# Combining the experts' rows earlier and reordering the context's last layer in a two-block transformer

## The chip, the cores and the metric

The kernel runs on one core of a Trainium2 chip. The metric is the device time of one execution in microseconds (us). Everything is computed in float32 by splitting each operand into a high and a low part and adding three products, so each weight block is cast once (ScalarE) and its remainder taken once (VectorE, DVE) before TensorE (PE) uses it.

## The reference

Two blocks follow each other on 512 tokens of width 1024. The first ends with a mixture of experts: a router picks two of sixteen experts for each token, each expert is a gated feed-forward, and the two results are added with the token's weights.

```python
def expert_block(args):
    xblk, e = args
    return (jax.nn.silu(xblk @ w1[e]) * (xblk @ w3[e])) @ w2[e]
yb = lax.map(expert_block, (xb, blk_e)).reshape(P, D)
out = jnp.zeros((N + 1, D), f32).at[row_tok].add(yb.astype(f32) * row_w[:, None])
...
x = x + hierarchical_moe(h, ...)
return rms_norm(x, g_final)
```

The second block has two layers over these 512 tokens and a context of 256 tokens. Each layer projects the latent tokens and the context with the same weights, mixes by three kinds of attention (neighbourhood attention, gated linear attention, grouped-query attention), and adds a feed-forward. The latent tokens need the context's keys, values and final states of the same layer. After the last layer the context itself is not needed, so in it the context yields keys, values and states alone:

```python
for l in range(DEPTH_2):
    ctx_out = l < DEPTH_2 - 1
    ...
    if ctx_out:
        xc = layer_norm(...)   # attention and feed-forward of the context
return x
```

## The kernel before, in words

The context doesn't depend on the first block. `moe` (L1164) therefore runs two instruction streams side by side: the foreground is the context's layer 0 (`layer2(0, stc, None, True)`, L1187), the background is a Python generator `experts` (L1177) that routes and then computes the sixteen experts. Each time the foreground has prepared a weight block (`wchunk`, L385), `pump` (L318) advances the background by `rate` steps, 1.85 here; a step of an expert is one 512 KB weight block with its six matmuls, and an expert has twelve. What the generator's steps and the foreground emit is the order of the program; the tile framework then issues instructions by readiness with that order as priority, waits for tiles that are still in use, and keeps each engine's queue in order.

The two streams have their own weight buffers: the experts four raw blocks and three split blocks, the context's layer 0 two and two (`Stream("c", ring, 2, 2, 2, 2, 512)`, L1185). The feed-forward of the context (`ffn`, L2101) has 66 weight blocks: for each of the first two factors 22 blocks of 128 hidden columns, and 22 blocks of the output projection, in groups of 4, 4, 4, 4, 2 and 4 times 128 hidden columns. Its layer norm follows the last block; `hT_tile` (L490) transposes the rows, applies scale and shift and splits them.

Then the context's layer 1 (`layer2(1, stc, None, False)`, L1196) runs as the foreground, with `combine` (L1201) behind it as the background at one step per weight block. `combine` loads the four row tiles of the tokens on SyncE's queue (SP), gathers each token's two expert rows from DRAM (eight indirect transfers on GpSimd's queue), adds them on DVE (`add`, L1221), takes the norm on ScalarE, writes the transposed tile of the main stream (`rest`, L1228), multiplies the rows on GpSimd and stores them on SP's queue. The gathers read `yd`, so they wait for the last expert's store (L1454).

In layer 1 the context runs, in the order of the program: gated linear attention (`gla`, L1830: gate projection, decay chain with exponentials, logarithms and scans, keys, values, states), grouped-query keys (128 columns) and values (128 columns) in two projections (L1721, L1723), neighbourhood values (`na_v`, L1577), and three blocks of neighbourhood keys (`na`, `na_kq`). Keys, values and states are stored to DRAM for the main stream, on SP's queue. Then the main stream's layer 0 begins with the gate projection of its own `gla`.

Tiles that matter: `pj` is a projection of tokens, `pf` of features, `fab` the feed-forward's first two factors, `h` and `yps` an expert's products, `raw`, `w_h`, `w_l` a weight block and its parts, `hT_h` and `hT_l` transposed inputs, `yg` a gathered row tile, `xmoe` the tokens' rows, `gfin` a row of gains.

## Time and profile before

| | |
|---|---|
| median of 3 runs | 2645.08 us (2640.8 to 2653.45) |
| the profiled execution | 2653.58 us, of which its span is 2651.8 us |
| PE busy | 2481.3 us, 94% |
| DVE busy | 1700.1 us, 64% |
| ScalarE busy | 1281.5 us, 48% |
| DMA | 436.54 MB, 165 GB/s on average |
| mean granted clock of PE | 0.963 of full |

A matmul's busy time overlaps with its neighbour's; the distance from start to start is what one costs. The clock that the throttle grants PE has two levels, 1.2 and 2.4 GHz, and a stretch's number is the mean of both over it. A releaser in brackets is the wait that came last before an instruction that found its engine idle.

### The profile page before, as it was taken

The page shows a single profiled execution, that of the slowest core. Times are in us where ns is not written, and L with a number is a line of the kernel's source. Part 1 is how long each engine was busy: PE and PEld are TensorE (multiplying, and loading weights), DVE is VectorE, ACT ScalarE, POOL GpSimd, SP SyncE. Part 2 cuts the span into 40 slices and gives each one's busy share as a digit, 9 for nine tenths or more (in the row PEclk, how much of TensorE's full clock was granted, in tenths as well). Part 3 has the DMA queues.
Part 4 walks back from the last instruction along what each step waited for, and adds up shares of the span by engine and source line. Part 5 has one row for each costly group of instructions (what it writes and reads, how often), then busy time and mean ns, then how long its engine had stood idle before and what let it go on. Part 6 is the DMA issues. An engine that isn't in the chain of part 4 may idle for free.

```text
span 2651.8 us, 35923 instructions
## 1 busy us (share of the span) xinstructions
PE 2481.3 (94%) x13176; PEld 1962.2 (74%) x13176; DVE 1700.1 (64%) x3145; ACT 1281.5 (48%) x2389; POOL 359.2 (14%) x306
## 2 busy tenths in 40 slices
PE   8899899888898999989989999999989899999997
PEld 5547575667677888877876588888868766888886
DVE  3355645787777777877876565444567876644446
ACT  4343445477755665656757642222266574422221
POOL 1100000110001000012230023111142300421101
PEclk9999899899999999988999999999989899999999
DMA  7764347489787898867254224333323524233331
GB/s 276 210 215 147 124 163 269 136 271 302 265 280 242 272 300 279 272 234 224 57 160 128 91 66 127 96 96 99 102 88 97 156 77 135 66 104 100 96 96 64
DMA packets 354132, 436.54 MB, mean 165 GB/s; under 512 B 20384, under 2 KB 228128, under 8 KB 353952
## 3 DMA queue, kind: packets, MB, share of 16 engines
q1 hardware_dynamic: 348000, 412.70, 48.9%
q0 software_dynamic: 5952, 21.50, 2.6%
q8 instruction: 105, 1.72, 0.3%
q14 instruction: 75, 0.61, 0.1%
HBM read 387.21 MB, written 38.01 MB: 160 GB/s over the span
## 4 chain that ended last, share of the span: by engine, by line
PE 46%; DVE 4%; ACT 2%; issue 1%; POOL 1%; DMA 1%; DVEq 0%; ACTq 0%; POOLq 0%
PE fab L345 18%; PE pj L345 17%; PE oat L637 3%; PE pf L345 3%; PE ptp L577 2%; PE sc L544 1%; PE sc L545 1%; PE glG L1983 1%; DMA nab<-in_nabias 1%; POOL x L2081 0%; PE tp L502 0%; DVE w_l L353 0%; ACT pga L663 0%; POOL x L2080 0%; ACT ht L510 0%
## 5 line engine op out<-in xcount | busy, mean ns | idle before, releaser
L353 DVE TENSOR_TENSOR w_l<-raw,w_h 128x1024 fp32r<-128x1024 f32 (+2 forms) x530 | 682.8, 1296 | 452.2 <-ACT w_h L352 443.3
L352 ACT CAST w_h<-raw 128x1024 fp32r<-128x1024 f32 (+2 forms) x530 | 528.3, 1005 | 824.8 <-PE pj L345 279.2
L345 PE MATMUL fab<-hTf_h,w_h 128*128 128x512 f32 (+1 forms) x1104 | 382.4, 348 | 3.6 <-ACT hTf_h L516 3.0
L345 PE MATMUL fab<-hTf_l,w_h 128*128 128x512 f32 (+1 forms) x1104 | 382.7, 347 | 0.2
L345 PE MATMUL fab<-hTf_h,w_l 128*128 128x512 f32 (+1 forms) x1104 | 382.7, 348 | 0.2 <-DVE w_l L353 0.2
L345 PE MATMUL pj<-w_l,hT_h 128*128 128x512 f32 (+3 forms) x608 | 228.7, 377 | 11.3 <-DVE w_l L353 11.3
L345 PE MATMUL pj<-w_h,hT_h 128*128 128x512 f32 (+3 forms) x608 | 221.6, 376 | 12.7 <-ACT w_h L352 7.7
L345 PEld LDWEIGHTS fab<-hTf_h,w_h 128*128 128x128 f32 x1104 | 209.7, 190 | 32.1 <-ACT hTf_h L516 3.4
L345 PEld LDWEIGHTS fab<-hTf_h,w_l 128*128 128x128 f32 x1104 | 209.6, 190 | 28.0 <-DVE w_l L353 0.4
L345 PEld LDWEIGHTS fab<-hTf_l,w_h 128*128 128x128 f32 x1104 | 209.8, 190 | 27.7 <-DVE hTf_l L517 0.6
L345 PE MATMUL pj<-w_h,hT_l 128*128 128x512 f32 (+3 forms) x608 | 224.5, 371 | 0.0
L389 POOL TENSOR_TENSOR raw<-raw,g2b 128x1024 f32<-128x1024 f32 x44 | 113.5, 2588 | 478.7 <-DMA raw<-in_w_ffn_out 437.9
L345 PEld LDWEIGHTS pj<-w_h,hT_h 128*128 128x128 f32 x608 | 119.0, 198 | 42.7 <-issue 14.3
L345 PEld LDWEIGHTS pj<-w_l,hT_h 128*128 128x128 f32 x608 | 120.8, 199 | 39.4 <-DVE w_l L353 16.5
L345 PE MATMUL pj<-w_l,wk_h 128*128 128x512 f32 x376 | 146.2, 390 | 0.5 <-DVE w_l L353 0.5
L345 PE MATMUL pj<-w_h,wk_h 128*128 128x512 f32 x376 | 145.3, 390 | 0.2 <-DVE gps L2072 0.2
L345 PE MATMUL pj<-w_h,wk_l 128*128 128x512 f32 x376 | 143.5, 390 | 0.0
L345 PE MATMUL pf<-hT_h,w_h 128*128 128x512 f32 (+3 forms) x376 | 132.3, 353 | 7.9 <-ACT pT L579 2.9
L345 PEld LDWEIGHTS pj<-w_h,hT_l 128*128 128x128 f32 x608 | 120.6, 198 | 20.9 <-issue 5.2
L345 PE MATMUL pf<-hT_l,w_h 128*128 128x512 f32 (+3 forms) x376 | 130.4, 347 | 2.0 <-DVE hT_l L517 2.0
L345 PE MATMUL pf<-hT_h,w_l 128*128 128x512 f32 (+3 forms) x376 | 130.2, 347 | 0.0
L579 ACT COPY pT<-ptp 128x512 f32<-128x512 f32 (+3 forms) x184 | 88.1, 498 | 55.0 <-PE ptp L577 53.9
(602 smaller groups left out, 4845.5 us busy)
## 6 DMA issues: line engine op xcount, KB each, us to landing
raw<-in_w SPq DMA_DIRECT2D x192, 512.0 KB
raw<-in_w_ffn_in SPq DMA_DIRECT2D x132, 512.0 KB
raw<-in_w_ada SPq DMA_DIRECT2D x96, 512.0 KB
raw<-in_w_in SPq DMA_DIRECT2D x76, 512.0 KB
raw<-in_w_ffn_out SPq DMA_DIRECT2D x66, 512.0 KB
raw<-in_w_out SPq DMA_DIRECT2D x32, 512.0 KB
yd<-ysb SPq DMA_DIRECT2D x16, 512.0 KB
raw<-in_w_in SPq DMA_DIRECT2D x16, 384.0 KB
```

The source lines that it names most:

```text
L345: self.nc.tensor.matmul(out, lhsT=l, rhs=r, start=first and k == 0 and i == 0, stop=last and k == n - 1 and i == 2, **kw)
L352: nc.scalar.copy(out=hl.hi, in_=src)
L353: nc.vector.tensor_sub(out=hl.lo, in0=src, in1=f32(hl.hi))
L389: self.nc.gpsimd.tensor_tensor(out=raw, in0=raw, in1=row.unsqueeze(1).to_broadcast([P, kt, n]), op=OP.mult)
L544: self.nc.tensor.matmul(o, lhsT=q, rhs=k.hi, start=True, stop=False)
L545: self.nc.tensor.matmul(o, lhsT=q, rhs=k.lo, start=False, stop=True)
L577: self.behind = nc.tensor.transpose(tp[:, b * P:(b + 1) * P], st["p"][:, (b0 + b) * P:][:, :P], self.ident)
L579: nc.scalar.copy(out=pT()[:, slice(b0, b0 + bb), ts], in_=tp[:, :bb * P].rearrange("p (b t) -> p b t", t=P))
L637: self.nc.tensor.matmul(st["o"][64 * hh:64 * hh + 64, cols_], lhsT=v(hh), rhs=pT(hh), start=n == 0, stop=n == len(terms) - 1, skip_group_c ...
L1983: nc.tensor.matmul(G[w * c:w * c + w, g0:g0 + GL_H * w].rearrange("p (h t) -> p h t", t=w), lhsT=xk[:, k0:k0 + w], rhs=qb[:, i, :, q0:q0 + ...
```

## The change

The diff does four things. `combine` becomes the tail of the experts' generator: its row loads go to GpSimd's queue, its rows lie in the buffers of the experts' inputs and its gathered rows in `hg` and a small new pool, and additions, norm and the first scaling happen there. The rest (`block2_input`: transposed tiles, multiplication, stores, the last on GpSimd's queue) stays behind the context's layer 1, beginning with the eleventh step. While a background runs, the rate in the feed-forward rises from 1.85 to 2.3. For the context's last layer the order becomes neighbourhood values, neighbourhood keys, the gates of `gla` up to the scans, grouped-query keys and values (called from within `gla`), then the keys, values and states of `gla`. And in that layer the grouped-query keys and values come from one projection of 256 columns. Other layers keep their order.

```diff
@@ -1180,6 +1180,7 @@
                 for e in range(NEXP):
                     yield from self.expert(hd, idx[:, e:e + 1], A["w1"][e], A["w3"][e], A["w2"][e],
                                            yd[e * P:(e + 1) * P, :], ep)
+                yield from self.combine(st, yd, posi, ew, ep)
             ex = Stream("", self.ring, 4, 3, 2, 1, 1024, parts=self.wparts)
             with self.background(ex, experts(), 1.85):
                 self.S = Stream("c", ring, 2, 2, 2, 2, 512)
@@ -1189,8 +1190,7 @@
         self.core_tile(st, 4)
         with self.mirrored():
             with self.psum("psc"):
-                with tc.tile_pool(name="moec", bufs=1, side="left", reuse_waits="tile") as cp, \
-                        self.background(Stream("c", None, 0, 0, 2, 0, 0), self.combine(st, yd, posi, ew, ep, cp), 1.0):
+                with tc.tile_pool(name="moec", bufs=1, side="left", reuse_waits="tile") as cp,                         self.background(Stream("c", None, 0, 0, 2, 0, 0), self.block2_input(st, cp), 1.0):
                     self.S = Stream("", self.ring, 4, 3, 4, 2, 512, parts=self.wparts)
                     self.pump()
                     ctxd.append(self.layer2(1, stc, None, False, keep_hT=True))
@@ -1198,42 +1198,52 @@
         self.S = self.main
         return ctxd
 
-    def combine(self, st, yd, posi, ew, ep, cp):
+    def combine(self, st, yd, posi, ew, ep):
+
+        nc, tc = self.nc, self.tc
+        xs = st["xs"] = []
+        with tc.tile_pool(name="moey", bufs=1, side="left", reuse_waits="tile") as cy:
+            ys = []
+            for i in range(4):
+                x = ep.tile([P, D], F32, name="x", tag=("ehT_h", "ehT_l")[i // 2], bufs=2)
+                nc.gpsimd.dma_start(out=x, in_=st["xd"][i * P:(i + 1) * P, :])
+                xs.append(x)
+            for i in range(4):
+                for k in range(2):
+                    pool, tag = ((ep, "hg"), (cy, "yg"))[i % 2]
+                    y = pool.tile([P, D], F32, name="yg", tag=tag, bufs=2)
+                    nc.gpsimd.indirect_dma_start(out=y, out_offset=None, in_=yd,
+                                                 in_offset=bass.IndirectOffsetOnAxis(ap=posi[k][:, i:i + 1], axis=0))
+                    ys.append(y)
+                yield
+                if i > 0:
+                    self.combined(i - 1, xs, ys, ew)
+            yield
+            self.combined(3, xs, ys, ew)
+
+    def combined(self, i, xs, ys, ew):
+        x = xs[i]
+        for k in range(2):
+            self.nc.vector.scalar_tensor_tensor(out=x, in0=ys[2 * i + k], scalar=ew[k][:, i:i + 1], in1=x, op0=OP.mult, op1=OP.add)
+        r = self.rms_rstd(x.unsqueeze(1), 1, junk=ys[2 * i])
+        self.nc.scalar.mul(x, x, r)
+
+    def block2_input(self, st, cp):
 
         nc = self.nc
         s, t = self.mod_cols(st["ada"][0][1], 1, 0, 0, self.c("vpack", "g_final"), None, "md0", self.cst)
+        g = self.bcast_row(cp, 1, "gfin")
         xd = self.dr.tile([T1, D], F32, name="xd")
-        xs, ys = [], []
+        xs = st["xs"]
+        for _ in range(10):
+            yield
         for i in range(4):
-            x = cp.tile([P, D], F32, name="x", tag="x", bufs=4)
-            nc.sync.dma_start(out=x, in_=st["xd"][i * P:(i + 1) * P, :])
-            xs.append(x)
-            for k in range(2):
-                tag, bufs = (("hg", 2), ("hg", 2), ("ehT_h", 2), ("ehT_h", 2), ("ehT_l", 2), ("ehT_l", 2), ("ysb", 1))[len(ys)] \
-                    if len(ys) < 7 else ("yg", 1)
-                y = (ep if len(ys) < 7 else cp).tile([P, D], F32, name="yg", tag=tag, bufs=bufs)
-                nc.gpsimd.indirect_dma_start(out=y, out_offset=None, in_=yd,
-                                             in_offset=bass.IndirectOffsetOnAxis(ap=posi[k][:, i:i + 1], axis=0))
-                ys.append(y)
+            self.hT_tile(xs[i], i, st["hT"], s, t, cp)
+            yield
+        for i in range(4):
+            nc.gpsimd.tensor_tensor(out=xs[i], in0=xs[i], in1=g, op=OP.mult)
+            nc.gpsimd.dma_start(out=xd[i * P:(i + 1) * P, :], in_=xs[i])
         st["xd"] = xd
-        g = self.bcast_row(cp, 1, "gfin")
-
-        def add(i):
-            x = xs[i]
-            for k in range(2):
-                nc.vector.scalar_tensor_tensor(out=x, in0=ys[2 * i + k], scalar=ew[k][:, i:i + 1], in1=x, op0=OP.mult, op1=OP.add)
-            r = self.rms_rstd(x.unsqueeze(1), 1, junk=ys[2 * i])
-            nc.scalar.mul(x, x, r)
-
-        def rest(i):
-            self.hT_tile(xs[i], i, st["hT"], s, t, cp)
-            nc.gpsimd.tensor_tensor(out=xs[i], in0=xs[i], in1=g, op=OP.mult)
-            nc.sync.dma_start(out=xd[i * P:(i + 1) * P, :], in_=xs[i])
-        for _ in range(6):
-            yield
-        for f, i in ((add, 0), (add, 1), (rest, 0), (add, 2), (rest, 1), (add, 3), (rest, 2), (rest, 3)):
-            f(i)
-            yield
 
     def overflow(self, hd, yd, posf, ovi, pool, ep):
 
@@ -1718,9 +1728,19 @@
             t = sq()
             nc.scalar.activation(t, qk[:, i], AF.Square)
             nc.vector.reduce_sum(ss[:, i * nh:(i + 1) * nh], t, axis=AX.X)
-        self.proj_tok(hT, nt, W[:, c0:c0 + nh * 64], ev)
         v = keep.tile([P, nt, P], F32, name="gav")
-        self.proj_tok(hT, nt, W[:, 2464:2592], lambda i, c0, n, ps: self.copy(v[:, i, :], ps[:, :n]))
+
+        def ev_v(i, _, n, ps):
+            self.copy(v[:, i, :], ps[:, :n])
+
+        def ev_kv(i, _, n, ps):
+            ev(i, _, P, ps)
+            ev_v(i, _, P, ps[:, P:])
+        if full:
+            self.proj_tok(hT, nt, W[:, c0:c0 + nh * 64], ev)
+            self.proj_tok(hT, nt, W[:, 2464:2592], ev_v)
+        else:
+            self.proj_tok(hT, nt, W[:, c0:2592], ev_kv)
         mid = between()
         r = self.rsqrt(ss, nt * nh, 1.0 / 64, 1e-6).rearrange("p (t h) -> p t h", h=nh)
         if full:
@@ -1827,7 +1847,7 @@
             return units
         return attend, mid
 
-    def gla(self, l, hT, T, W, ctxd, full, d, late, pool):
+    def gla(self, l, hT, T, W, ctxd, full, d, late, pool, within):
 
         nc, A = self.nc, self.A
         nt = T // P
@@ -1862,6 +1882,8 @@
         reset = self.c("cpack", "reset")[:, :T]
         nc.vector.tensor_tensor_scan(bs[0], reset, bs[0], 0.0, OP.mult, OP.add)
         nc.vector.tensor_tensor_scan(bs[1][:, ::-1], reset, bs[1][:, ::-1], 0.0, OP.mult, OP.add)
+        if not full:
+            within()
         q = pool.tile([P, T], F32, name="glq")
         k = pool.tile([P, T], F32, name="glk")
 
@@ -2165,15 +2187,22 @@
             hT = lambda k: hTt[:, k, :]
             nes = ExitStack()
             g0, bias = {}, []
-            with tpool("gqp") as p2, tpool("gll") as p0:
+            with tpool("gqp") as p2, ExitStack() as pes:
+                if not full:
+                    vd = self.na_v(l, hT, T, W, p2)
+                    with tpool("nap") as p:
+                        self.na(l, hT, T, W, ctxd, full, d, vd, p, p, g0, (), bias)
+                p0 = pes.enter_context(tpool("gll"))
                 with tpool("glp") as p1:
-                    finish = self.gla(l, hT, T, W, ctxd, full, d, p0, p1)
+                    finish = self.gla(l, hT, T, W, ctxd, full, d, p0, p1,
+                                      lambda: self.gqa(l, hT, T, W, ctxd, full, d, keep, p2, lambda: None, iter(())))
                 p3 = nes.enter_context(tpool("na0", side=self.far)) if lat else None
                 if lat:
                     self.na_bias(l, p3, bias)
                     g0["kc"] = self.fetch(ctxd["na_k"][0], p3, "nakc", bufs=2)
                 begun = self.na_kq(0, l, hT, T, W, lat, full, p3, g0, d) if lat else iter(())
-                attend, vd = self.gqa(l, hT, T, W, ctxd, full, d, keep, p2, lambda: self.na_v(l, hT, T, W, p2), begun)
+                if full:
+                    attend, vd = self.gqa(l, hT, T, W, ctxd, full, d, keep, p2, lambda: self.na_v(l, hT, T, W, p2), begun)
                 self.call(finish)
             oes = ExitStack()
             rows, cols_ = st["ada"][l]
@@ -2209,12 +2238,12 @@
                     self.pipeline(units + [(lambda: switch(s0), *rest)] + more, steps=5)
                 gr, lg, lb = lnr
             else:
-                with tpool("nap") as p:
-                    self.na(l, hT, T, W, ctxd, full, d, vd, p, p, g0, begun, bias)
                 if not full:
                     if not keep_hT:
                         st["hes"].close()
                     return d
+                with tpool("nap") as p:
+                    self.na(l, hT, T, W, ctxd, full, d, vd, p, p, g0, begun, bias)
                 with tpool("gqa") as p:
                     self.pipeline(attend(oT, p))
         with tpool("xx") as px:
@@ -2273,6 +2302,9 @@
                     self.affine(x[:, i, :], x[:, i, :], lg, lb)
                     nc.sync.dma_start(out=xd[i * P:(i + 1) * P, :], in_=x[:, i, :])
                 later = []
+                if self.bg is not None:
+
+                    self.rate = 2.3
                 self.ffn(l, lambda k: hTf[:, k, :], T, x, gr, wk, done2)
                 if later:
                     self.behind_input(st["hT"], lp, later)
```

## Rows read from the trace of the kernel before

**Rows 1.** Page: busy time by engine; granted TensorE clock in 40 equal slices
```profile
PE 2481.3 (94%) x13176; PEld 1962.2 (74%) x13176; DVE 1700.1 (64%) x3145; ACT 1281.5 (48%) x2389; POOL 359.2 (14%) x306
PEclk9999899899999999988999999999989899999999
```

**Rows 2.** Windows: length, engine busy (instructions), PEclk, DMA share, GB/s
```profile
813.80:1152.65 338.85, 337.18 (x2011) 297.03 (x2009) 264.15 (x299) 201.21 (x249) 6.11 (x6) 1.00 0.84 276
1152.65:1169.12 16.47, 9.10 (x45) 6.78 (x43) 15.03 (x40) 9.13 (x17) 0.00 (x0) 0.90 0.57 178
1169.12:1182.40 13.28, 11.59 (x76) 10.37 (x76) 3.97 (x6) 2.43 (x5) 7.66 (x8) 0.86 0.95 329
1182.40:1206.80 24.40, 21.11 (x97) 20.43 (x97) 20.64 (x55) 17.80 (x37) 0.42 (x1) 0.51 0.40 128
1206.80:1239.16 32.36, 27.24 (x192) 25.35 (x193) 32.10 (x68) 22.54 (x45) 14.10 (x8) 1.00 0.76 228
```

**Rows 3.** Waits of PE, 1152.65 to 1239.2: us in total, times, longest
```profile
PE pj L345 <- DVE w_l L353: 4.9, 4, 2.1
PE tp L502 <- DVE x L2061: 4.1, 1, 4.1
PE pf L345 <- ACT hT_h L516: 2.1, 1, 2.1
PE pf L345 <- DVE hT_l L517: 2.0, 1, 2.0
PE pj L345 <- issue: 1.7, 1, 1.7
```

**Rows 4.** Timeline of PE (start, duration, shape): one pair of neighbours per shape and clock
```profile
1184.42 0.41 PE L345 MATMUL pj<-w_h,hT_l 128*128 128x256 f32 x1
1184.64 0.41 PE L345 MATMUL pj<-w_h,hT_h 128*128 128x256 f32 x1
1195.23 0.41 PE L345 MATMUL pj<-w_l,hT_h 128*128 128x128 f32 x1
1195.44 0.41 PE L345 MATMUL pj<-w_h,hT_l 128*128 128x128 f32 x1
...
1208.84 0.27 PE L345 MATMUL pj<-w_l,hT_h 128*128 128x128 f32 x1
1208.95 0.28 PE L345 MATMUL pj<-w_h,hT_l 128*128 128x128 f32 x1
...
1214.96 0.34 PE L345 MATMUL pj<-w_l,hT_h 128*128 128x384 f32 x1
1215.13 0.33 PE L345 MATMUL pj<-w_h,hT_l 128*128 128x384 f32 x1
1226.07 0.28 PE L345 MATMUL pf<-hT_l,w_h 128*128 128x256 f32 x1
1226.19 0.28 PE L345 MATMUL pf<-hT_h,w_l 128*128 128x256 f32 x1
```

**Rows 5.** DVE groups, 1152.65 to 1241.2: xcount, busy, mean ns; one meeting with POOL
```profile
L1224 DVE SCALAR_TENSOR_TENSOR x<-yg,ew,x 128x1024 f32<-128x1024 f32 x8 | 10.1, 1278 | 0.5 <-DMA yg<-yd,posi 0.5
...
1206.38 2.36 POOL L1230 TENSOR_TENSOR x<-x,gfin 128x1024 f32<-128x1024 f32 x1 [24.84 <-ACT yg L487]
1206.84 1.92 DVE L470 SCALAR_TENSOR_TENSOR rqa<-rqz,rqv 128x1 f32<-128x1 f32 x1
```

**Rows 6.** Timelines of SP, ACT and DVE: one 512 KB weight block, issue to split
```profile
1248.34 1.14 SPq L382 DMA_DIRECT2D raw<-in_w_in  x2
1252.42 1.05 ACT L352 CAST w_h<-raw 128x1024 fp32r<-128x1024 f32 x1 [2.69 <-DMA raw<-in_w_in]
1253.50 1.23 DVE L353 TENSOR_TENSOR w_l<-raw,w_h 128x1024 fp32r<-128x1024 f32 x1 [3.12 <-ACT w_h L352]
```

**Rows 7.** Timeline of SP: the last expert's store
```profile
1162.06 0.36 SPq L1454 DMA_DIRECT2D yd<-ysb  x1
```

**Rows 8.** POOL groups, 813.8 to 1152.65: the experts' gathers
```profile
L1423 POOL DMA_INDIRECT hg<-hd,idx x6 | 6.1, 1018 | 237.6 <-PE etp L1429 156.4 <-PE h L345 46.0 <-DMA raw<-in_w 35.1
```

## Prediction

> **What bounds the kernel now.** I read the page first: TensorE (PE) is busy for 94% of the span and the other engines for much less, so only time in which PE idles or runs slowly can be won, apart from PE work that is deleted [rows 1]. In the clock line two 8s stand side by side in one place only, slices 18 and 19, 1127 to 1260 us, which hold the end of the experts and the context's last layer [rows 1]. That part I cut by stage [rows 2]. In the first stretch the experts and the context's layer-0 feed-forward run side by side; PE is busy for 337.18 of 338.85 us at full clock, and the DMA engines are 84% busy. There nothing is to be had except less PE work. From 1152.65, where the context's last feed-forward matmul has run, to 1239.16, where the main stream's projections run without a gap, 86.51 us pass in four stages. The layer-norm tail leaves PE 9.10 of 16.47 us of work. Then the combine's traffic fills the DMA engines (0.95, 329 GB/s) for 13.28 us. Then 24.40 us run with a mean clock of 0.51, so nearly all of it at 1.2 of 2.4 GHz. In the last 32.36 us the clock is full again and VectorE (DVE) is busy for 32.10. The waits name who was late [rows 3]: weight splits on DVE, the layer norm, the context's and the main stream's transposed inputs.
>
> **The change, part by part.**
>
> Merged keys and values. One projection of 128 columns less: 8 blocks of k x 2 token tiles x 3 terms = 48 matmuls go, since 96 of 128 columns become 48 of 256. The pairs of neighbours [rows 4] give the spacing: 128 columns take 0.11 us at full clock and 0.21 at half, 256 columns 0.12 and 0.22. The merged form costs as much per matmul as the narrow one. So 5.3 us go at full clock, 10.1 at half. Four weight blocks, their loads, casts and DVE splits go too; these lie beside PE, so I cost them at nothing.
>
> Combine leaves the context's last layer. There its eight additions hold DVE for 10.1 us [rows 5], its four row loads and eight gathers make the DMA-full stage [rows 2], and behind that traffic the values' weights came late: PE waits 1.7 and, for splits, 4.9 us [rows 3], and the clock falls. All of this goes into the experts' chain.
>
> Reordered last layer. Token-major values come first (they can start on token tile 0 while tile 1 is still normalised), then three key blocks, then gates, gated keys and values with the merged projection in between. The same work moves, but the gates' chain of table functions and scans now has 48 matmuls beneath it, and the main stream's four transposed tiles are free to go earlier, as their rows are ready: the 2.0 us wait on them [rows 3] goes.
>
> The stretch after, summed on PE by the spacings of [rows 4] at full clock: neighbourhood values 48 x 0.17 = 8.2; neighbourhood keys 72 x 0.12 = 8.6; gate projection 24 x 0.12 = 2.9; merged 48 x 0.12 = 5.8; gated keys 24 x 0.12 = 2.9; gated values 48 x 0.12 = 5.8; the main stream's 32 transposes and the small matmuls of the gates and states, at 0.11 each, some 7. That is 41 us. Ahead of it stands the tail. It took 16.47 us with the last expert's splits, copy and matmuls in between [rows 2], whose DVE part I estimate at four to five weight-size operations of 1.23 us [rows 6]; without them I take 10.5 (bounds 8 and 14). The idle tail lowers the clock as before, so I add 2.5 us for a slow start. DVE then has the last four windows' 71.7 us [rows 2] less 10.1 for the additions, some 5 for the four reciprocal-root chains and 5 for the experts: 51 us. That fits in a stretch of 58, but tightly, so I keep 4.5 us of PE waits (bounds 0 and 12). Together 41 + 10.5 + 2.5 + 4.5 = 58.5, against 86.51: 28.0 us gained (bounds 18 and 33).
>
> The experts' last product now runs earlier. Its 24 matmuls of 512 columns and four transposes lie between 1152.65 and 1160; they filled the tail. Of the tail's 9.10 us of PE work [rows 2] I put 6 on them. They move into a stretch in which PE is full, so they cost their length: -6.0.
>
> The rate of 2.3. Counting yields and weight blocks in the code, 88.8 of the experts' 200 steps are due when the feed-forward begins. At 1.85 per block the other 111 end at block 60 of 66; at 2.3 at block 48. In the trace the last expert's store comes at 1162.06, behind the context's last matmul [rows 7], so the experts run some 6 blocks behind their due place; I expect their end near block 54, and 12 blocks of feed-forward without them. Those blocks have only two raw buffers. A cycle of one buffer is 4.1 us from issue to cast, 1.05 cast, 1.23 split, about 0.3 between, 6.7 together [rows 6], so 3.35 us per block; PE needs 24 x 0.12 = 2.9 us. Loss 12 x 0.45 = 5.4. Meanwhile the combine moves 4 x 0.5 + 8 x 0.5 = 6.3 MB; with 6.3 MB of own weights and 1.6 MB of the next layer's first blocks that is 14.2 MB, 43 us at the 329 GB/s of [rows 2], against 35 us of PE: 8 us at most. The two overlap, so I take 6 (bounds 0 and 12, and more in a rival). While experts run, 3.3 blocks per 6.3 us instead of 2.85 per 5.6 raise the load by 3%, from 276 to about 285 GB/s, still under 329: nothing.
>
> Row loads and stores on GpSimd's queue. SP no longer issues four loads and four stores; GpSimd issues them behind the last gather of the experts, which needs them no more. Behind a store there wait only the main stream's tables and bias loads, due 10 us later: nothing. The row multiplications on GpSimd stay, and with them the stalls of DVE (an operation on one column took 1.92 us beside one [rows 5]).
>
> The trace's six expert gathers took 1.02 us each on GpSimd while DVE was 78% busy [rows 2, 8]; eight combine gathers beside an idle DVE are no quicker, 7.66 us in all [rows 2]. The Trainium skill, page "SBUF — State Buffer", section "SBUF: two separate sides", speaks against the move: DVE and GpSimd hold a shared port exclusively, and a transfer from GpSimd's queue can starve for descriptors while DVE holds it. By that rule the four loads and four stores that move to this queue would land late and the additions with them, which is rival 3's time; by the rows they won't, and the sum stands.
>
> Sum: -28.0 + 6.0 + 6.0 = **16 us less**. The profiled execution took 2653.58 us (span 2651.8); 2637.6 on its own scale. It lies 8.5 above the median of 2645.08, so the forecast is 2629.
>
> **The rivals.** (1) The gain is eaten: DVE sets the new stretch (58.5 grows to 66, since it had 51 us of work in a chain of small steps) and the unaccompanied blocks lose 12. -20.5 + 6 + 12 = -2.5: 2643. For it: DVE's 32.10 of 32.36 us in the last stage [rows 2].
>
> (2) Slower: in the feed-forward without experts the two buffers open a gap at every block, and the clock falls as it did behind the short gaps before 1184 [rows 3, 4]. At 0.22 us a block takes 5.2 instead of 2.9 us; without a lag 17.7 blocks are alone, 17.7 x 2.3 = 40 us. -28 + 6 + 40 = +18: 2663. It decides once the blocks alone lose over 22 + 13 = 35 us. Against it: over 1169.12 to 1182.40, right behind the idle tail and with matmuls of 256 columns, the mean clock was 0.86 [rows 2], so it came back there; and weights may be fetched ahead.
>
> (3) The change doesn't do what it says: the rows' buffers are those of the experts' inputs, and every gather needs the last expert's store; if the experts lag to the end as they do now, the additions still fall into the last layer. The merged projection and the end wait remain: -5.3 - 2.0, 2638. The skill's rule on the shared port would push the same way; its landing delays would add to the lag.
>
> **How the numbers follow.** Forecast 0.60 (its own range 2613 to 2643), rival 1 0.18, rival 2 0.09, rival 3 0.13. This kernel's measurement can tell about 0.5%, 13.2 us, from no change, so faster means below 2631.9. The forecast lies just past it and gives 0.42 to faster and 0.18 to within; rival 3 gives 0.03 and 0.10; rival 1 0.01 to faster, 0.16 within, 0.01 slower; rival 2 all to slower. Together faster 0.46, same 0.44, slower 0.10. The range from 2612 to 2651 takes in the bounds of the stretch and both middle rivals and leaves out rival 2.
>
> **What would show it.** Right: between the context's last feed-forward matmul and the main stream's first about 58 us, no narrow 128-column projection at half clock, no wait on the main stream's transposed input, the additions before the tail. Wrong: PE gaps of some 0.5 us at every block after the last expert, with the clock below full there (rival 2); additions behind the tail (rival 3); DVE full through the new stretch with PE waiting on splits (rival 1). If the tail takes over 14 us, or the DMA engines are full in the feed-forward while the experts still run, the sum is wrong too.

## The result and the profile after

The changed kernel takes 2678.3 us (median, 2676.36 to 2684.44), the kernel before 2648.47 beside it: ratio 1.0118, interval 1.0101 to 1.0135, some 30 us slower. The forecast was 2629, its range 2612 to 2651. The profiled execution took 2678.12 us, its span 2676.3.

The page of after, the lines that answer to [rows 1] (busy time by engine; TensorE's busy tenths and granted clock in 40 slices of 67 us):

```profile
PE 2465.5 (92%) x13128; PEld 1947.4 (73%) x13128; DVE 1698.9 (63%) x3141; ACT 1285.7 (48%) x2387; POOL 361.9 (14%) x314
...
PE   8999899898889999946998999999989899999997
...
PEclk9999899898999999978999999999999899999999
```

TensorE (PE) has 48 instructions and 15.8 us of busy time less: the merged projection is there. But slices 18 and 19 (1137 to 1271 us) now hold a 4 and a 6. The windows of after, columns as in [rows 2]; the first runs from the context's last feed-forward matmul to its layer 1's first matmul, the others from there to the main stream's first matmul at 1272.83:

```profile
1163.10:1201.67 38.57, 5.07 (x22) 3.80 (x21) 25.21 (x69) 12.86 (x20) 8.56 (x8) 0.56 0.56 176
1201.67:1207.00 5.33, 5.17 (x21) 4.67 (x20) 3.00 (x6) 2.76 (x6) 0.00 (x0) 0.65 0.00 0
1207.00:1220.00 13.00, 13.00 (x99) 12.96 (x98) 10.22 (x15) 8.70 (x16) 3.00 (x2) 1.00 0.51 146
1220.00:1232.00 12.00, 11.81 (x103) 11.35 (x101) 6.47 (x14) 6.00 (x16) 3.03 (x3) 1.00 0.71 203
1232.00:1244.50 12.50, 4.21 (x12) 2.59 (x12) 9.72 (x22) 7.60 (x16) 2.88 (x2) 0.67 0.92 297
1244.50:1256.40 11.90, 0.00 (x1) 0.03 (x1) 7.44 (x21) 10.57 (x19) 6.74 (x12) 0.50 0.12 49
1256.40:1272.83 16.43, 13.90 (x86) 12.41 (x87) 8.40 (x18) 5.33 (x11) 0.00 (x0) 0.81 0.65 193
```

PE stands in three places: 38.57 us with 5.07 busy, 12.50 with 4.21, and 11.90 with nothing. PE's waits from 1150 to 1280 (us in total, times, longest), the answer to [rows 3], name them:

```profile
PE tp L502 <- DVE rqz L465: 32.0, 1, 32.0
PE gtp L1805 <- DVE gf L1798: 12.0, 1, 12.0
PE tp L502 <- ACT ht L510: 10.0, 2, 8.4
```

None of the waits in [rows 3] is left above 0.2 us; three longer ones stand in their place. The first is the layer norm behind the context's layer 0, whose end PE's transposes need. SP, GpSimd (POOL) and VectorE (DVE) in that time show why it is late (start, duration, what ended the idle time before it):

```profile
1165.77 0.36 SPq L1464 DMA_DIRECT2D yd<-ysb  x1
...
1170.53 0.99 POOL L1215 DMA_INDIRECT yg<-yd,posi  x1 [21.96 <-issue]
...
1178.73 0.94 POOL L1215 DMA_INDIRECT yg<-yd,posi  x1 [3.44 <-DVE x L1227]
...
1167.13 0.68 DVE L2072 BATCH_NORM_STATS2 bst<-x 128x6 f32<-128x512 f32 x1
1174.93 1.28 DVE L1227 SCALAR_TENSOR_TENSOR x<-yg,ew,x 128x1024 f32<-128x1024 f32 x1 [7.12 <-DMA yg<-yd,posi]
...
1190.13 1.28 DVE L1227 SCALAR_TENSOR_TENSOR x<-yg,ew,x 128x1024 f32<-128x1024 f32 x1
...
1193.82 0.20 DVE L2077 BATCH_NORM_AGGREGATE bmv<-bst 128x2 f32<-128x12 f32 x1
```

The context's statistics are done at 1167.81. The next instruction in DVE's queue is the experts' first addition. It needs a gather, and every gather needs the last expert's store of 1165.77 (before: 1162.06 [rows 7]). Four gathers go out at 1170.5 to 1175.3; the next four find no free buffer until the first additions are done. So all eight additions and four chains of reciprocal roots pass ahead of the layer norm, which is ready and goes on 26 us later.

Set against the forecast's own steps (us; "before" from [rows 2]):

| stage | before | forecast | after |
|---|---|---|---|
| end of the context's last feed-forward matmul | 1152.65 | +12 | 1163.10, +10.45 |
| tail, to layer 1's first matmul | 16.47 | 10.5, -6.0 | 38.57, +22.1 |
| layer 1, to the main stream's first | 70.04 | 48, -22.0 | 71.16, +1.1 |
| all behind it | 1412.6 | 0 | 1403.5, -9.2 |
| span | | -16 | +24.5 |

I take the last step as no effect of the change: in the profiles of all the kernels below this remainder lies between 1402 and 1415, also where the combine was left alone, and the profiled run of before was 5.1 us above the median beside it. Without that step the loss is 33.7, near the 30 of the medians.

### The profile page after: what moved, and what is told of

It is laid out like the page before. It is cut to its first block, busy times and chain, and to the rows that moved or that the text cites. A ratio compares the mean times of both kernels' runs of the same rounds, so it can differ in the third digit from the quotient of the medians.

```text
span 2676.3 us, 35806 instructions
## 1 busy us (share of the span) xinstructions
PE 2465.5 (92%) x13128; PEld 1947.4 (73%) x13128; DVE 1698.9 (63%) x3141; ACT 1285.7 (48%) x2387; POOL 361.9 (14%) x314
## 2 busy tenths in 40 slices
DMA packets 353044, 436.52 MB, mean 163 GB/s; under 512 B 20321, under 2 KB 227041, under 8 KB 352865
## 4 chain that ended last, share of the span: by engine, by line
PE 57%; DVE 6%; ACT 3%; DMA 3%; issue 2%; POOL 1%; SPq 0%; DVEq 0%; ACTq 0%; POOLq 0%
PE fab L345 22%; PE pj L345 19%; PE h L345 3%; PE pf L345 3%; PE oat L637 3%; PE yps L345 2%; DVE w_l L353 2%; PE ptp L577 2%; PE sc L544 1%; ACT w_h L352 1%; PE sc L545 1%; PE glG L2005 1%; DMA nab<-in_nabias 1%; DMA raw<-in_w_ffn_out 1%; DMA raw<-in_w 1%
## 5 line engine op out<-in xcount | busy, mean ns | idle before, releaser
L353 DVE TENSOR_TENSOR w_l<-raw,w_h 128x1024 fp32r<-128x1024 f32 (+3 forms) x526 | 681.7, 1304 | 458.1 <-ACT w_h L352 454.5
L352 ACT CAST w_h<-raw 128x1024 fp32r<-128x1024 f32 (+3 forms) x526 | 526.6, 1012 | 834.4 <-PE pj L345 271.6
L345 PE MATMUL pj<-w_h,hT_h 128*128 128x512 f32 (+3 forms) x592 | 214.1, 372 | 11.3 <-ACT w_h L352 7.8
L345 PE MATMUL pj<-w_l,hT_h 128*128 128x512 f32 (+3 forms) x592 | 218.3, 369 | 5.6 <-DVE w_l L353 5.6
L345 PE MATMUL pj<-w_h,hT_l 128*128 128x512 f32 (+3 forms) x592 | 214.5, 365 | 0.0
L345 PEld LDWEIGHTS pj<-w_h,hT_h 128*128 128x128 f32 x592 | 112.3, 191 | 38.9 <-ACT w_h L352 8.9
L345 PEld LDWEIGHTS pj<-w_l,hT_h 128*128 128x128 f32 x592 | 113.0, 191 | 31.2 <-DVE w_l L353 9.6
L345 PEld LDWEIGHTS pj<-w_h,hT_l 128*128 128x128 f32 x592 | 112.8, 191 | 20.5 <-issue 5.2
```

The lines of the kernel that those rows point to most:

```text
L345: self.nc.tensor.matmul(out, lhsT=l, rhs=r, start=first and k == 0 and i == 0, stop=last and k == n - 1 and i == 2, **kw)
L352: nc.scalar.copy(out=hl.hi, in_=src)
L353: nc.vector.tensor_sub(out=hl.lo, in0=src, in1=f32(hl.hi))
```

## The experiments

All medians and ratios to the kernel before, with two times of the profiled run: the longest wait of PE's transposes in the tail, and the time from the first matmul of layer 1 to the main stream's first. (In the kernel before, the 70.0 end at the main stream's second matmul, which waits 2.0 us for its input [rows 3]; to the first it is 67.6.)

| kernel | median us | ratio, interval | wait | layer 1 |
|---|---|---|---|---|
| before | 2645 to 2648 | 1 | 4.1 | 70.0 |
| after | 2678.3 | 1.0118 (1.0101 to 1.0135) | 32.0 | 71.2 |
| e1_rate185 | 2683.0 | 1.0138 (1.0110 to 1.0165) | 34.6 | 72.0 |
| e2_old_combine | 2648.9 | 1.0009 (0.9994 to 1.0024) | 4.1 | 75.5 |
| e3_comb_only | 2679.0 | 1.0129 (1.0100 to 1.0158) | 30.3 | 64.8 |
| e4_merge_only | 2661.1 | 1.0051 (1.0028 to 1.0073) | 4.1 | 76.9 |
| e5_no_wait | 2663.2 | 1.0071 (1.0047 to 1.0094) | 13.3 | 71.2 |
| e6_late_additions | 2665.4 | 1.0082 (1.0063 to 1.0102) | 5.8 | 73.2 |
| e7_reorder_only | 2650.0 | 1.0020 (1.0006 to 1.0033) | 4.1 | 74.1 |
| e8_keys_gpsimd | 2684.7 | 1.0146 (1.0130 to 1.0161) | 32.7 | 72.9 |
| e9_keys_after_values | 2666.5 | 1.0078 (1.0063 to 1.0093) | 32.0 | 65.2 |
| e10_late_both | 2662.0 | 1.0068 (1.0054 to 1.0082) | 5.3 | 74.6 |
| e11_old_combine_both | 2655.6 | 1.0039 (1.0023 to 1.0056) | 4.1 | 81.6 |
| e12_no_merge | 2681.7 | 1.0145 (1.0120 to 1.0170) | 31.0 | 72.6 |
| e13_no_reorder | 2680.3 | 1.0127 (1.0101 to 1.0154) | 29.7 | 63.3 |
| e14_no_tables | 2678.8 | 1.0132 (1.0109 to 1.0155) | 31.1 | 69.4 |
| e15_comb_only_late | 2667.1 | 1.0086 (1.0067 to 1.0104) | 5.3 | 69.3 |
| e16_no_tables_no_gpsimd | 2675.2 | 1.0104 (1.0075 to 1.0134) | 31.7 | 66.0 |
| e17_no_gpsimd | 2680.6 | 1.0136 (1.0108 to 1.0164) | 29.5 | 72.4 |
| e18_before_no_gpsimd | 2645.9 | 0.9998 (0.9979 to 1.0018) | 4.1 | 68.6 |

### Which part of the change costs

e1 takes one line out of the changed kernel:

```diff
-                if self.bg is not None:
-                    self.rate = 2.3
```

> The changed kernel without the line that raises the rate to 2.3 (1.85 throughout). Theory: the rate does not set the experts' pace, since TensorE was full and the last expert's store came at 1165.77 us with 2.3 and at 1162.06 with 1.85; so the time stays within 4 us of the changed kernel's 2678 (2674 to 2682) and the last store within 5 us of 1165. Rival: the rate counts, and without it the last store falls behind the context's feed-forward by some 10 us or more, the additions later still: 2685 or more.

2683.0, 1 us over the theory's range and the same as after within the intervals. The last store came at 1157.77, not later but 8 us earlier than at 2.3 (and 4 earlier than before): my 5 us were too narrow, and the rival is refuted. Five of the 8 us lie ahead of the context's feed-forward, which begins at 807.04 in e1 and at 812.28 in after. Counted from there the last store comes at 350.7 us at 1.85 and at 353.5 at 2.3 (before: 348.3). So the higher rate doesn't bring the experts' end forward.

It does put off the end of the feed-forward. At 2.3, 19 of the 24 matmuls of the last expert's product run ahead of the feed-forward's last matmul; at 1.85, in e1 as in before, all 24 run behind it. The windows from the feed-forward's first to its last matmul, of after and then of e1, columns as in [rows 2] (before: 338.85, 337.18 busy):

```profile
812.28:1163.10 350.82, 344.38 (x2033) 302.54 (x2032) 267.33 (x302) 204.43 (x254) 9.30 (x10) 0.99 0.84 276
807.04:1148.48 341.44, 337.41 (x2010) 297.15 (x2009) 262.85 (x298) 200.53 (x249) 8.30 (x10) 1.00 0.86 279
```

As long as the additions hold the layer norm until the last store has landed, these 9.4 us don't show in the time.

e2, e3, e4 and e7 give the kernel before one or two of the diff's parts: the reordering and the merge; the combine's move with its rate; the merge; the reordering.

> The kernel before with the reordered last layer and the merged keys and values, but with the combine where it was, behind the last layer's weight blocks. Theory: the main loss is the additions that stand in VectorE's queue ahead of the context's final layer norm (TensorE idle for 32.0 us); they are gone here, so that wait is under 12 us, the two queue stalls of the reordered layer (8.4 and 12.0 us) are still seen, and the time is 2645 to 2658. Rival: the reorder alone makes the loss; then the time is 2668 or more. Second rival, the forecast's own sum of the reorder: 2640 or less.

> The kernel before with the combine in the experts' chain and the rate of 2.3, but with the old order of the last layer and two projections. Theory: the additions ahead of the layer norm cost TensorE 25 to 32 us of idle time at the end of the context's layer 0, of which some 10 to 15 come back because the last layer is free of them: 2655 to 2672. Rival, the reorder is the loss and the move of the combine a gain: 2640 or less.

> The kernel before with the one projection for grouped-query keys and values alone. Theory: 48 matmuls go, which ran at half clock before: 5 to 10 us less than before, 2638 to 2644. Rival: what bounds that stretch are the late weights and splits, not the matmuls, so the time is that of before within 2 us.

> The kernel before with the reordered last layer alone: two projections, combine where it was. The runs so far gave 2649 for reorder and merged projection together and 2661 for the merged projection alone, against 2647 before. Theory: the two add up, so the reorder alone gains 12: 2630 to 2642. Rival: they don't add up, the merged projection costs only in the old order, where its weights come behind the combine's transfers, and the reorder alone changes nothing: 2644 to 2651. Second rival: the reorder's queue stalls (8.4 and 12.0 us in the changed kernel) cost by themselves: 2655 or more.

e12 and e13 take one part out of the changed kernel: the merged projection, the new order.

> The changed kernel with two projections of 128 columns in place of the merged one. So far, with the additions early: neither reorder nor merge 2679, both 2678; with the additions late in the last layer: neither 2647, reorder 2650, merge 2661, both 2649. Theory: the stretch of the last layer is set by a chain of gates, norms and evacuations through ScalarE and VectorE, not by TensorE's matmuls, so 48 more of them cost nothing: within 4 us of the changed kernel, 2674 to 2682. Rival: TensorE's matmuls set it and their 5 to 10 us come on top: 2684 to 2688.

> The changed kernel with the old order of the last layer, so the additions in the experts' chain, rate 2.3 and the merged projection. Theory: the two queue stalls of the new order (8.4 and 12.0 us) are not seen, but the merged projection costs in the old order as it did alone: 2674 to 2690. Rival: the merge costs only beside the combine's transfers; with these gone the 5 to 10 us of deleted matmuls show, on top of the 2679 without it: 2668 to 2674.

Together they fill a table of all three parts:

| combine | neither | merge | reorder | both |
|---|---|---|---|---|
| in the last layer | 2647 | 2661 | 2650 | 2649 |
| in the experts' chain | 2679 | 2680 | 2682 | 2678 |

The move of the combine costs 29 to 32 us in three of the four columns and 19 beside the merge alone: it is the loss, with the rate of 2.3 that comes with it. e2's time and its short wait behind the norm are the theory's, though of the two stalls of the new order it has 7.0 and 2.8 us where I expected 8.4 and 12.0. e3's theory holds for the wait, but I had expected 10 to 15 us back from a last layer free of additions, and its time lies above the 2655 to 2672 that I gave. PE's waits of e3, 1150 to 1280:

```profile
PE tp L502 <- DVE rqz L465: 30.3, 1, 30.3
PE pf L345 <- DVE nak_l L353: 3.3, 1, 3.3
PE tp L502 <- ACT ht L510: 2.3, 2, 1.5
```

Here the two stalls of the new order are not there, and layer 1 takes 64.8 us instead of 70.0: that is all that the combine's leaving returns.

With the combine early, the merge and the order make no difference that the runs can tell. e12's theory holds, at its upper edge: 48 matmuls more cost nothing that shows. e13's time is the theory's too, but the merge cost nothing there, and the keys' wait stayed at 8.7 us in the old order, so that stall belongs to the merge as much as to the new order. The merge alone in the old order misses both of e4's expectations: 14 us slower, not 5 to 10 faster. Of these 14 us the window of layer 1 in e4 shows 6.8 (before: 59.94 busy of 70.04):

```profile
1166.25:1243.12 76.87, 51.34 (x314) 47.05 (x315) 60.30 (x128) 44.18 (x86) 26.27 (x22) 0.79 0.71 228
```

PE works 8.6 us less and waits 15.4 us more. Its profiled run (2648.12) was the shortest of its runs, so the rest of the 14 us stays open. e7's sum doesn't add up either: the reorder alone gains nothing (2650, its first rival); it only makes the merge harmless.

### The wait for the additions

e5 keeps everything of the changed kernel but the gathers' source:

```diff
-                    nc.gpsimd.indirect_dma_start(out=y, out_offset=None, in_=yd, ...)
+                    nc.gpsimd.dma_start(out=y, in_=st["xd"][i * P:(i + 1) * P, :])
```

> The changed kernel whose eight row gathers are plain loads of the tokens' own rows, which need no expert's store; the experts' results are so left out of the sum, the additions, norms and their place in the program stay. Theory: what TensorE waits for in its 32.0 us is VectorE, which holds the layer norm behind additions that wait for the last expert; without that wait the idle time is 8 to 14 us and the time 2652 to 2662. Rival, the additions' own work and the norm chain make the wait: it stays over 25 us and the time over 2670. If the sum of the forecast for the last layer holds as well once the additions are early, the time is 2620 to 2640.

e6 keeps the instructions and changes the order:

```diff
                     ys.append(y)
-                yield
+                if i == 1:
+                    for _ in range(400):
+                        yield
                 if i > 0:
                     self.combined(i - 1, xs, ys, ew)
-            yield
             self.combined(3, xs, ys, ew)
```

> The changed kernel with the same instructions, but the additions put behind the layer norm in the order of the program (the combine waits 400 steps ahead of its first addition, so the rest of it comes when the context's layer 0 is written out). Theory: the wait of 32.0 us falls under 12 us, the additions and the second four gathers lie beside the last layer's projections, and the time is that of the run with the old combine, 2640 to 2656. Rival: the additions are on the path of the main stream's transposed inputs wherever they stand, so 2665 or more.

e5: the wait falls from 32.0 to 13.3 and the time to 2663.2, 15 us less, 1 us over the theory's range. Its layer 1 takes 71.2 us, as in after, so the forecast's 48 fail with or without that wait. PE's waits of e5 and then of e6:

```profile
PE tp L502 <- DVE rqz L465: 13.3, 1, 13.3
PE gtp L1804 <- DVE gf L1797: 11.7, 1, 11.7
PE tp L502 <- ACT ht L510: 9.8, 2, 8.3
```

```profile
PE tp L502 <- ACT ht L510: 15.9, 4, 6.6
PE gtp L1806 <- DVE gf L1799: 9.3, 2, 7.9
PE tp L502 <- DVE rqz L465: 5.3, 1, 5.3
```

So DVE's queue is the cause of this part, by two ways of undoing it: no wait in front of the additions, or the layer norm in front of them. Both give back 13 to 15 us and no more. In e6 the wait for the norm falls to 5.3 as expected, but its time is the rival's, 2665.4, and the next additions come between the evacuations of the layer norm's transposes, on the same queue:

```profile
1169.12 0.80 DVE L2084 TENSOR_SCALAR x<-x,bmv,rqz 128x1024 f32<-128x1024 f32 x1
1172.90 1.28 DVE L1228 SCALAR_TENSOR_TENSOR x<-yg,ew,x 128x1024 f32<-128x1024 f32 x1 [2.98 <-DMA yg<-yd,posi]
1174.11 0.72 DVE L514 TENSOR_SCALAR ht<-tp,md1s,md1t 128x128 f32<-128x128 f32 x2
```

The evacuation that PE waits for (L514) stands behind an addition that waits 2.98 us for its gather. Layer 1's first matmul comes at 1180.21, against 1168.41 in e2, where the last expert's product, 24 matmuls, runs after the context's last one and fills part of the tail. In the changed kernel, e5 and e6 most of that product lies among the feed-forward's last blocks. PE in e6, behind its last feed-forward matmul (1161.00):

```profile
1167.63 1.97 PE L502 MATMUL tp<-cpack,x 128*128 128x128 f32 x8 [5.32 <-DVE rqz L465]
1175.40 1.12 PE L502 MATMUL tp<-cpack,x 128*128 128x128 f32 x4 [5.80 <-ACT ht L510]
1179.44 1.12 PE L502 MATMUL tp<-cpack,x 128*128 128x128 f32 x4 [2.92 <-ACT ht L510]
```

So e6's tail of 19.2 us still holds the combine's additions. In after and in e5 layer 1's first matmul follows 5.3 us behind the first transposes. With that and the 6.6 us up to the transposes here, I estimate a tail without additions and without the product at 11.9 us. Where the product runs in the tail (e2, e7) it is 15.0.

What e6 loses against e2 (16.5 us by the medians) is in the traces 11.2 us of a longer feed-forward (351.95 against 340.71) and 4.2 of tail. The first goes with the rate of 2.3, as between after and e1. Late additions with the rate of 1.85 were not run, so how much of the 16.5 us the rate alone costs stays open.

e15 gives e3 the late additions:

> The kernel before with the combine in the experts' chain and the rate of 2.3, old order, two projections, but with the additions put behind the layer norm in the order of the program. Theory: as in the changed kernel this takes away 13 to 20 of the 31 us lost; the rest is the layer norm's tail, no longer covered by the last expert's product: 2655 to 2668. Rival, the old order lets the last layer keep its shorter stretch (65 us) as well: 2640 to 2650.

2667.1, 12 us less than e3, within the theory's range. Its layer 1 takes 69.3 us, not 65: as with e6, part of the additions now lies in it.

### What holds the last layer

e8 sends the neighbourhood keys' copies and stores of the last layer to GpSimd's queue; e9 calls the grouped-query projection behind the gated values:

```diff
-            d["na_k"].append(self.spill(k, f"nakc{l}{f}"))
+            d["na_k"].append(self.spill(k, f"nakc{l}{f}", None if full else nc.gpsimd))
```

```diff
-        if not full:
-            within()
         q = pool.tile([P, T], F32, name="glq")
...
             self.proj_tok(hT, nt, W[:, 1408:1664], lambda i, c0, n, ps: self.copy(v[:, i, :], ps[:, :n]))
+            within()
```

> The changed kernel with the neighbourhood keys' copies and stores of the context's last layer on GpSimd's queue, so that SP can issue the next weights at once. Theory: the wait of 8.4 us (TensorE's transposes behind ScalarE's evacuations, these behind a weight cast whose load SP issued late, after the key stores) falls under 3 us; 4 to 8 us less than the changed kernel: 2670 to 2674. Rival: the load itself or ScalarE is what is late, and the wait stays: 2676 to 2683.

> The changed kernel with the grouped-query keys and values behind the gated keys and values, no longer between the gates and them. Theory: the wait of 12.0 us is one of order, since two transposes stand in TensorE's queue ahead of projections that are ready, and their norm chain stands in VectorE's queue behind additions that wait for ScalarE's gates; it falls under 4 us and the time is 2666 to 2672. Rival: the gates' chain on ScalarE is what everything waits for, and the wait appears elsewhere (at the states' matmuls): 2675 to 2683.

The reason for e8 is in the trace of after: SP issues 17 key copies and stores (L535, L370) from 1217.47 to 1229.78, with one weight block between them and the next behind; ScalarE (ACT) waits for these with the evacuations in its queue, and PE for the evacuations:

```profile
1229.83 0.45 SPq L382 DMA_DIRECT2D raw<-in_w_in  x1
...
1235.84 1.04 ACT L352 CAST w_h<-raw 128x1024 fp32r<-128x1024 f32 x1 [3.55 <-DMA raw<-in_w_in]
```

In e8 that wait falls from 8.4 to 4.9, but the sum of PE's waits doesn't: 12.0 becomes 8.6, and 9.3 appear ahead of the states (PE waits of e8; then of e9):

```profile
PE tp L502 <- DVE rqz L465: 32.7, 1, 32.7
PE gltp L1930 <- DVE glt L1926: 9.3, 1, 9.3
PE gtp L1805 <- DVE gf L1798: 8.6, 1, 8.6
PE tp L502 <- ACT ht L510: 8.0, 3, 4.9
```

```profile
PE tp L502 <- DVE rqz L465: 32.0, 1, 32.0
PE gltp L1929 <- DVE glt L1925: 13.0, 2, 11.6
PE tp L502 <- ACT ht L510: 2.0, 2, 1.5
```

e8's theory falls (2684.7, just over the rival's range). e9's time, 2666.5, is the theory's, 12 us less than after, but for another reason: the wait of 12.0 is replaced by 13.0 at the gates' keys, as its rival had it, while the 8.4 us behind the late weights go and the stretch shrinks to 65.2. Its profiled feed-forward also ended 7 us earlier (at 1156.17, having begun 10 us earlier), which is nothing that the edit touches, so I credit the edit with the 6 us of the stretch.

e10 puts e6, e8 and e9 together, e11 the edits of e8 and e9 on e2.

> The changed kernel with the late additions and both edits of the two runs beside this one. Theory: the three waits are three orders in queues and their prices add up: 13 for the additions as measured, 4 to 8 and 6 to 12 for the others, so 2645 to 2657. If that is all that was in the way of the forecast's sum, 2640 or less. Rival: what one wait gives back the next one takes, and the time stays at 2660 to 2668.

> The kernel before with the reordered last layer and the merged projection, the combine where it was, and both edits of the runs beside this one. Theory: the waits of 7.0 us (behind late weights) and of 2.8 us go in part: 2638 to 2645, a little faster than before. Rival: with the combine in the last layer VectorE and the transfers bound it, not the order: 2646 to 2652, as without the edits.

The prices don't add up. e10 takes 2662.0, 3 us less than e6: its rival. e11 is 7 us slower than e2, worse than either expectation, with PE's wait at the gates' keys again at 7.8.

e14 asks whether the gates' function tables hold the chain; e16 and e17 take GpSimd's work (row multiplications, rotation tables) to DVE, with and without the tables; e18 does that to the kernel before.

```diff
-            nc.scalar.activation(a, a, AF.Exp, scale=-1.0)
+            nc.scalar.activation(a, a, AF.Exp if full else AF.Copy, scale=-1.0)
```

```diff
-            nc.gpsimd.tensor_tensor(out=xs[i], in0=xs[i], in1=g, op=OP.mult)
+            nc.vector.tensor_tensor(out=xs[i], in0=xs[i], in1=g, op=OP.mult)
```

> The changed kernel whose gates in the context's last layer use copies in place of exponentials and logarithms, so that ScalarE loads no function tables there; that part of the computation is left out. Theory: the last layer is bound by the chain through ScalarE and VectorE; without four to five table loads of 1.28 us the wait of 12.0 us falls to 5 to 8 and the time by 4 to 7 us: 2670 to 2675. Rival: the order of VectorE's and TensorE's queues alone sets it, and the wait stays over 10 us, the time within 3 us of 2678.

> The run without table loads (the gates' exponentials and logarithms in the last layer are copies, left out of the computation), and with the row multiplications and the rotation tables on VectorE instead of GpSimd. Theory: table loads on ScalarE and GpSimd's hold on VectorE are two limits beside each other, so that either alone hides the other; with both gone the scan takes under 1 us, the wait of 11.5 us falls under 6 and the time by 4 to 8 us: 2670 to 2675. Rival: the order of the queues sets the wait, it stays over 10 us, and VectorE's added work makes it 2678 to 2684.

> The changed kernel with the row multiplications and the rotation tables on VectorE instead of GpSimd, all else as it is. Theory: the table loads alone still hold the gates' chain, so the wait stays at 10 to 13 us and the time within 4 us of the changed kernel: 2674 to 2683. Rival: GpSimd's hold on VectorE is what counts; the wait falls under 7 us and the time to 2668 to 2674.

> The kernel before with the row multiplications and the rotation tables on VectorE instead of GpSimd. GpSimd's four multiplications take 2.3 us each, in which small operations of VectorE took 1.9 us; on VectorE they should take 1.2 us each. Theory: VectorE is the fuller engine in the last layer's end, so 3 to 8 us less than before: 2637 to 2643. Rival: the stalls lie beside other waits and nothing changes: 2644 to 2649; or the added 5 us of VectorE work come on top: 2649 to 2654.

Without table loads the wait of 12.0 us stayed at 11.5 and the time at 2678.8: the rival's numbers, but not its reason. DVE and GpSimd in e14, in the time of that wait:

```profile
1241.92 2.39 DVE L1883 TENSOR_TENSOR gla_b<-gla_b,gla_a 128x256 f32<-128x256 f32 x1
...
1244.64 4.17 DVE L1886 TENSOR_TENSOR_SCAN gla_b<-cpack,gla_b 128x256 f32<-128x256 f32 x1
...
1241.70 2.33 POOL L1244 TENSOR_TENSOR x<-x,gfin 128x1024 f32<-128x1024 f32 x1 [9.06 <-PE tp L502]
...
1244.94 0.73 POOL L1759 TENSOR_TENSOR tcq<-cpack,vpack 128x256 f32<-128x256 f32 x1
1245.62 1.14 POOL L1765 TENSOR_TENSOR tsq<-cpack,vpack 128x64 f32<-128x64 f32 x4
1246.72 0.71 POOL L1759 TENSOR_TENSOR tck<-cpack,vpack 128x256 f32<-128x256 f32 x1
1247.40 1.52 POOL L1765 TENSOR_TENSOR tsk<-cpack,vpack 128x64 f32<-128x64 f32 x4
```

The first, a subtraction, takes 2.39 us (0.42 in after), the scan 4.17 (0.81 in after): the one ends 0.29 us behind GpSimd's multiplication, the other 0.55 behind the ninth of GpSimd's ten table operations. In after most of that GpSimd work lay beside DVE's waits for the gates on ACT, with one small operation of DVE at 1.01 us. So two limits lie side by side, and taking one away uncovers the other. e16 takes both away: the scan takes 0.69 us, the wait falls to 7.4, layer 1 to 66.0. e17 takes GpSimd's alone: 12.4 and 72.4. The waits go the way of the theory of two limits (7.4 where I gave under 6); of the times, e16's 2675.2 has an interval that holds no gain as well. e18 changes nothing (its first rival, by which these stalls lie beside other waits in the kernel before; that reason isn't shown). No kernel here beats the one before.

## Why the prediction was wrong

**Where the experts end.** I expected their end near block 54, from counting steps at a rate of 2.3. They ended with the feed-forward, at 1.85 as at 2.3 (e1). The loss that I put on blocks without experts, 6 us, had nothing to occur in; PE's waits for weights in the whole feed-forward come to 3.6 us, so rival 2 fell with it. That the feed-forward took 12.0 us more (350.82 against 338.85), as the sum had it with 6 and 6, is luck: 7.2 are PE's work, and in 4.8 more it stands idle.

**The additions.** This is the first step that failed. The sum let them leave the last layer at no cost, and rival 3, which had them late, priced this at 2638: it asked where the additions fall, and not what stands behind them in DVE's queue. There stood the layer norm that all of layer 1 waits for. The text even has the last store, the gathers' need of it and the lag of the experts. It asked what waits behind them on GpSimd's queue and on SP's, and not on DVE's. By the rows of after the norm stood ready for 26 us; undoing the order or the wait returned 13 to 15 us of the time (e5, e6), in both with some of the additions still in the tail.

**The tail.** 10.5 us (bounds 8 and 14) stood in the sum, and after took 38.6. Without additions and product I estimate 11.9, so the term was right for the tail that it meant, and what it lacked are the additions. The product was priced wrongly: taken out of the tail, where it costs some 3 us (15.0 in e2 and e7 against 11.9, an estimate), it was to give back 6; ahead of it, it was to cost 6, where the feed-forward grew by 9.4 with the rate alone (e1 to after).

**The layer.** This is the second step that failed, and nearly as large. 41 us of PE work at full clock, 2.5 for a slow start and 4.5 for waits made 48. After took 71.2: 48.1 us of PE work and 23 us of waits, with a mean clock of 0.79 over both. The waits were the mis-sized term, five times my value and twice its bound. Rival 1 had the mechanism, that small steps on DVE set the stretch, and gave tail and layer together 66; they took 109.7 in after and 92.4 in e6. Layer 1 alone lies between 63 and 82 in all the runs, whatever is merged or moved. PE's matmuls are not the limit there: 48 of them more (e12) cost nothing that shows. (The merge's four weight blocks went as issues, not as bytes: 436.54 MB before, 436.52 after.) What the runs show of the limit is a chain of gates and norms through ACT and DVE, in queues whose order lets one wait for another, with table loads and GpSimd's stalls side by side (e14, e16, e17); which order would be short in all of them isn't settled.

**The shared port.** I weighed it for the combine's transfers. The gathers took 0.94 to 1.54 us on GpSimd in after, against 1.02 for the experts' [rows 8], so the value from the rows held. They landed 4.1 to 6.2 us after their issue, where those before took 6.7 to 6.8; landing delays of the kind that the Trainium skill, page "SBUF — State Buffer", section "SBUF: two separate sides", makes possible are not seen in it. Where the two engines did meet is DVE's operations beside GpSimd's arithmetic, which I named with its 1.92 us [rows 5] and gave no price, as it stays.

## What to carry to other kernels

Before work is moved ahead of a stage, look in each in-order queue at what will stand behind its waiting instruction, the vector engine's first: one addition that waited for a transfer held back a layer norm that was ready, and TensorE waited 32.0 us. Work that fills a gap costs little there: moved out, it gives back little and costs at least its length where it goes. And where a stretch is a chain of small steps, deleted matmuls are worth nothing until the chain is shorter; when a wait goes, look which one has taken its place before crediting the edit.

## What the runs showed of the hardware

GpSimd can hold VectorE for longer than one instruction. In e14 the scan started 0.29 us ahead of ten GpSimd instructions in a row and stood at 4.17 us. Nine of the ten passed at 0.31 to 0.74 us each; the tenth took 0.69, where the three like it ahead took 0.31, and ended 0.11 us behind the scan. In e16, with that work gone, the scan took 0.69. The Trainium skill, page "SBUF — State Buffer", section "SBUF: two separate sides", has the two engines share a port as an exclusive lock, held for a whole instruction. The trace agrees that one blocks the other. That VectorE doesn't get the port between two GpSimd instructions, here not in eight chances, is more than the page states. It isn't always so: in after a small operation of VectorE (1.01 us, 0.15 elsewhere) was done behind the first of the same ten.

After PE's wait of 32.0 us the granted clock was 0.65 over 1201.67 to 1207.00, the first matmuls of layer 1, and then 1.00. It fell again in the wait of 8.4 us (1.00 over 1232.00 to 1235.50, 0.54 over 1235.50 to 1244.50) and stood at 0.50, its lower level, in the wait of 12 us. Before, with 24.4 us of narrow matmuls, it had stayed at 0.51 [rows 2].
